# The gate of the embedding as seven products of blocks, with the statistics of the first norm on ScalarE

## The chip, the cores and the metric

The kernel runs on one core of one Trainium2 chip. The metric is the device time of one execution in microseconds; the time of a kernel is the median of its runs. A core has a matrix engine (TensorE, PE in the profile; PEld is its loading of stationary operands), VectorE (DVE), ScalarE (ACT), GpSimd (POOL), and a queue of its own on SyncE (SP). Each engine works through its instructions in the order in which they stand; they wait for each other by semaphores. Transfers run on 16 DMA engines; they are issued here from SP (loads of weights) and POOL (sums of weights in DRAM, small tables, constants).

## The reference

One layer of a decoder on 512 tokens of width 1024, all in float32:

```python
def reference(x, p, w_in, ..., w_up, w_down, w_ple_gate, w_ple, ln2_g, ln2_b, rel_bias):
        m = mixer(x, ...)                                     # three attention branches, gated, projected
        x = layer_norm(DEEPNORM_ALPHA * x + m, ln1_g, ln1_b)  # the first norm
        hid = jax.nn.relu(x @ w_up)                           # 1024 to 4096
        c = jnp.square(hid) @ w_down
        ple = jax.nn.sigmoid(x @ w_ple_gate) * (p @ w_ple)    # the gate of the embedding
        x = layer_norm(DEEPNORM_ALPHA * x + c + ple, ln2_g, ln2_b)
```

The change is about `x @ w_ple_gate` (512 x 1024 times 1024 x 1024) and about the mean and variance of the first norm.

## The kernel before, in words

Every float32 product is made of three matmuls on rounded parts: an operand is split into a high part (a cast on ACT) and a low part (the difference, on DVE), and high x high, high x low and low x high are added up in PSUM. Weights come from DRAM in tiles of 128 x 1024 (512 KB): SP loads a raw tile into a ring of 7 (`fill`, line 179), ACT casts it (`split_next`, line 207), DVE subtracts (line 209) into a ring of 7 high and 7 low tiles. A tile is freed after its last matmul, and `pump` then issues the next splits.

The work is a list of items, written out by hand: each has its weight tiles, a function that issues matmuls into a PSUM bank, and an eviction that is issued with the next item. Between items a function `step` gives each open generator one turn: the attention heads first, later what is in `pending` (the norms and the forms of x). So the length of an item sets how often such a turn comes. The framework then orders the instructions of each engine; that order is fixed when the program is built.

The order of the items is: projections of x, the attention heads beside them, branch projections with their gates, the product of the embedding (`ple_items`), the output projection (`wout_items`, 651 to 697 us), the gate of the embedding (`pleg_items`, 697 to 742 us), and the MLP (`mlp_items`).

The output projection has eight items of 24 matmuls: two halves of the columns, and in each the four token tiles of 128 tokens. The eviction of an item adds the residual (DVE, line 497). After the second half of a token tile its first norm is put into `pending` (`ln1_gen`): statistics by BN_STATS and BN_AGGR on DVE (lines 437, 439), epsilon (441), the power -1/2 on POOL (442), then two passes over each half on DVE (444: subtract the mean and scale by the gain; 446: scale by the power and add the bias). At its next turn it issues eight transposes on TensorE (line 518); ACT evicts them as plain copies (`raws`, line 525) and as the high part of x transposed (line 526), and DVE makes the low part (line 527).

The second norm at the end of the kernel has another form, `layer_norm_act`: the eviction sums as it writes (`accum_out`, line 907), DVE makes the negative mean (454), ACT squares with the mean as its bias and sums (456), DVE scales and adds epsilon (458, 459), POOL takes the power (460), DVE makes the passes (462, 466).

The gate has eight items as well, two column halves by four token tiles, each of 8 x 3 = 24 matmuls of 128 x 128 by 512 columns (lines 564 to 566), with a sigmoid on ACT (570) and a product and a sum on DVE (571, 573). Token tile t is first needed by item t.

The up projection is made of seven products of blocks (of two by two blocks of x and of the weights) instead of eight. It needs sums of blocks of x, made by `x_forms` on DVE and split (lines 664 to 672, 654, 655), and sums of blocks of the weights, `usum`, which transfers in DRAM make beforehand (`sum_steps`, lines 621 and 623, eight steps for each group, issued from POOL). These are spread over the items: from item 24 on one or two an item, each tied to a weight split on DVE four splits back; after the output projection has begun, one every third item. POOL also issues, near 100 to 122 us, the small transfers of the bias tables (`tables`, lines 1011, 1020), which DVE reads later (`turned`, line 1030).

Of the kernel before, what the change touches and what calls it, by code (L numbers as in the profile page):

```python
# [56 lines left out]
def trunk(tc, a, out):  # L57
    nc = tc.nc
    es = ExitStack()
    with es:  # L60
# [99 lines left out]
        def chunk(src, w):  # L160
            return chunk_of(load(src, w))
# [256 lines left out]

        x1 = {}
        x1T = {}  # L420
# [12 lines left out]

        def layer_norm(ts, g, b, fin):
            s6 = one.tile([P, 2, 6], F32, name=nm("bn6"), tag="bn6", bufs=3)
            for h in range(2):
                nc.vector.bn_stats(s6[:, h, :], ts[h])
            mv = small("mv", 2)
            nc.vector.bn_aggr(mv, s6)
            r = small("lr", 1)  # L440
            nc.vector.tensor_scalar(r, mv[:, 1:2], EPS, None, op0=OP.add)
            nc.gpsimd.tensor_tensor(r, r, mhalf, OP.pow)
            for h in range(2):
                nc.vector.scalar_tensor_tensor(ts[h], ts[h], mv[:, 0:1], lnc[g][h], op0=OP.subtract, op1=OP.mult)
            for h in range(2):
                nc.vector.scalar_tensor_tensor(ts[h], ts[h], r, lnc[b][h], op0=OP.mult, op1=OP.add)
                fin(h, ts[h])
# [33 lines left out]
        def wout_items():  # L481
            for half in range(2):
                cs = [chunk(a["wo"][half, c].rearrange("p k n -> p (k n)"), 1024) for c in range(4)]
                for tt in range(4):
# [10 lines left out]
                    def ev(ps, tt=tt, half=half):  # L495
                        y = xn.pop((tt, half))
                        nc.vector.scalar_tensor_tensor(y, y, ALPHA, ps, op0=OP.mult, op1=OP.add)
                        x1[tt, half] = y
                        if half:
                            pending.append(ln1_gen(tt))  # L500
                    item(cs if tt == 3 else [], mm, ev, need=cs)

        def ln1_gen(tt):
            def fin(h, t):
                pass
            layer_norm([x1[tt, 0], x1[tt, 1]], "ln1_g", "ln1_b", fin)
            yield
            q = slice(tt * P, tt * P + P)
            if not x1T:
# [4 lines left out]
                x1T["b"], x1Tl["b"] = bh, bl  # L514
            for h in range(2):
# [4 lines left out]
                t3 = tp.rearrange("p (k t) -> p k t", k=4)  # L520
                for kp in range(2):
# [4 lines left out]
                nc.scalar.copy(o, t3)  # L526
                nc.vector.tensor_sub(x1Tl["b"][:, 4 * h:4 * h + 4, q], t3, o.bitcast(F32))
# [27 lines left out]
        def pleg_items():  # L555
            for half in range(2):
                cs = [chunk(a["wg"][half, c].rearrange("p k n -> p (k n)"), 1024) for c in range(4)]
                for tt in range(4):
                    def mm(ps, tt=tt, cs=cs):
                        for k in range(8):  # L560
                            c = cs[k // 2]
                            s = slice((k % 2) * 512, (k % 2) * 512 + 512)
                            q = slice(tt * P, tt * P + P)
                            nc.tensor.matmul(ps, x1T[k][:, q], c["h"][:, s], start=k == 0, stop=False)
                            nc.tensor.matmul(ps, x1T[k][:, q], c["l"][:, s], start=False, stop=False)  # L565
                            nc.tensor.matmul(ps, x1Tl[k][:, q], c["h"][:, s], start=False, stop=k == 7)  # L566

                    def ev(ps, tt=tt, half=half):
                        g = slot("sg2")
                        nc.scalar.activation(g, ps, AF.Sigmoid)  # L570
                        nc.vector.tensor_mul(g, g, ple.pop((tt, half)))
                        t = x1[tt, half]
                        nc.vector.scalar_tensor_tensor(t, t, ALPHA, g, op0=OP.mult, op1=OP.add)
                        acc[tt, half] = t
                    item(cs if tt == 3 else [], mm, ev, need=cs)
# [14 lines left out]
        ND = 8  # L590
# [1026 lines left out]
```

## Time and profile before

| what | us |
| --- | --- |
| median of three runs (1072.64 to 1073.74) | 1073.5 |
| the profiled execution | 1072.9 |
| its span, first to last instruction | 1071.2 |
| TensorE busy in it | 1060.4 |
| VectorE busy | 705.6 |
| ScalarE busy | 517.5 |
| GpSimd busy | 113.4 |

The profile tells for each engine when an instruction ran, on which line of the kernel it was issued, how long the engine stood idle before it and what ended that wait. A row of the time line has the start, the time from the first to the last of its instructions, the engine, the line, the operation, output and input, the count, and in brackets the idle time and what ended it. Matmuls overlap: a duration is a latency, and the distance between starts is what a matmul costs. Busy time of an engine is an average over stages with different limits.

### The profile page before, as it was taken

How to read it: one execution, taken by the hardware profiler on the slowest of the kernel's cores; microseconds unless marked ns; L12 is line 12 of the kernel's file. 1: busy time of each engine (PE TensorE's matmuls, PEld its weight loads, DVE VectorE, ACT ScalarE, POOL GpSimd, SP SyncE). 2: the span in 40 equal slices, each digit the busy share in tenths (PEclk: the TensorE clock that was granted, in tenths of full speed). 3: DMA queues.
4: the chain of work that ended last, by engine and by line, in shares of the span. 5: the costliest groups of instructions: out<-in, count | busy, mean ns of one | idle time of the engine just before them, and what ended most of it. 6: DMA issues, size and time to landing. Idle time of an engine off the chain costs nothing.

```text
span 1071.2 us, 14785 instructions
## 1 busy us (share of the span) xinstructions
PE 1060.4 (99%) x5562; PEld 910.4 (85%) x5562; DVE 705.6 (66%) x1262; ACT 517.5 (48%) x890; POOL 113.4 (11%) x175
## 2 busy tenths in 40 slices
PE   9999999999999999999999999999999999999996
PEld 6888788999888888888888888888999989989885
DVE  7888667547253757655444453895677877877965
ACT  7665545425232545554333331444765565665741
POOL 0000201011111002122120020110001010000000
PEclk9999999999999999999999999999999999999999
DMA  8332316183767419477897254245889788857502
GB/s 318 126 118 90 117 42 236 50 226 100 222 230 190 164 38 259 156 207 187 270 244 232 99 180 175 99 146 156 284 262 255 254 238 272 237 185 242 190 13 79
DMA packets 56199, 192.43 MB, mean 180 GB/s; under 512 B 7000, under 2 KB 7912, under 8 KB 56128
## 3 DMA queue, kind: packets, MB, share of 16 engines
q1 hardware_dynamic: 35904, 120.51, 32.4%
q0 software_dynamic: 19648, 70.06, 25.4%
q8 instruction: 43, 0.70, 0.3%
q10 hardware_dynamic: 576, 0.92, 0.2%
q14 instruction: 28, 0.23, 0.1%
HBM read 189.34 MB, written 65.04 MB: 237 GB/s over the span
## 4 chain that ended last, share of the span: by engine, by line
PE 96%; DVE 2%; ACT 0%; DMA 0%; issue 0%; SPq 0%; DVEq 0%
PE mm L88 16%; PE mm L89 16%; PE mm L90 16%; PE at L795 4%; PE at L796 4%; PE at L797 4%; PE mm L319 3%; PE mm L321 3%; PE mm L320 3%; PE at L90 1%; PE at L88 1%; PE at L89 1%; PE mm L566 1%; PE mm L493 1%; PE mm L491 1%; PE mm L565 1%
## 5 line engine op out<-in xcount | busy, mean ns | idle before, releaser
L207 ACT CAST wh<-raw 128x1024 fp32r<-128x1024 f32 (+1 forms) x225 | 232.2, 1034 | 310.1 <-PE mm L89 238.8
L209 DVE TENSOR_TENSOR wl<-raw,wh 128x1024 fp32r<-128x1024 f32 (+1 forms) x225 | 269.7, 1203 | 118.9 <-ACT wh L207 114.9
L88 PE MATMUL mm<-xhT,wh 128*128 128x512 f32 x496 | 196.4, 396 | 0.0
L89 PE MATMUL mm<-xlT,wh 128*128 128x512 f32 x496 | 194.0, 391 | 0.0
L90 PE MATMUL mm<-xhT,wl 128*128 128x512 f32 x496 | 194.0, 391 | 0.0
L90 PEld LDWEIGHTS mm<-xhT,wl 128*128 128x128 f32 x496 | 93.2, 188 | 19.6
L88 PEld LDWEIGHTS mm<-xhT,wh 128*128 128x128 f32 x496 | 93.3, 188 | 18.5 <-issue 0.2
L89 PEld LDWEIGHTS mm<-xlT,wh 128*128 128x128 f32 x496 | 93.2, 188 | 18.1 <-issue 0.2
L88 PE MATMUL mm<-x1hT,wh 128*128 128x256 f32 x256 | 73.8, 288 | 0.0
L795 PE MATMUL at<-wh,hh 128*128 128x512 f32 x188 | 73.7, 392 | 0.0
L796 PE MATMUL at<-wl,hh 128*128 128x512 f32 x188 | 73.7, 392 | 0.0
L797 PE MATMUL at<-wh,hl 128*128 128x512 f32 x188 | 73.1, 389 | 0.0
L89 PE MATMUL mm<-x1lT,wh 128*128 128x256 f32 x256 | 72.3, 283 | 0.0
L90 PE MATMUL mm<-x1hT,wl 128*128 128x256 f32 x256 | 71.8, 283 | 0.0
L319 PE MATMUL mm<-wh,xhT 128*128 128x512 f32 x160 | 64.6, 404 | 0.0
L321 PE MATMUL mm<-wh,xlT 128*128 128x512 f32 x160 | 63.1, 395 | 0.0
L320 PE MATMUL mm<-wl,xhT 128*128 128x512 f32 x160 | 62.9, 393 | 0.0
L88 PEld LDWEIGHTS mm<-x1hT,wh 128*128 128x128 f32 x256 | 48.8, 191 | 4.7 <-ACT up L729 2.9
L89 PEld LDWEIGHTS mm<-x1lT,wh 128*128 128x128 f32 x256 | 48.9, 191 | 1.5
L90 PEld LDWEIGHTS mm<-x1hT,wl 128*128 128x128 f32 x256 | 48.6, 191 | 0.0
L621 POOL DMA_DIRECT2D usum<-in_wu_dram x32 | 30.5, 962 | 157.5 <-DVE wl L209 152.7
L797 PEld LDWEIGHTS at<-wh,hl 128*128 128x128 f32 x188 | 35.3, 188 | 7.7
(372 smaller groups left out, 2170.1 us busy)
## 6 DMA issues: line engine op xcount, KB each, us to landing
raw<-in_wt_dram SPq DMA_DIRECT2D x62, 512.0 KB, 4.5
usum<-in_wu_dram POOLq DMA_DIRECT2D x48, 512.0 KB, 8.3
dsum<-in_wd_dram POOLq DMA_DIRECT2D x42, 512.0 KB, 8.5
raw<-usum SPq DMA_DIRECT2D x32, 512.0 KB, 4.7
raw<-dsum SPq DMA_DIRECT2D x28, 512.0 KB, 4.4
raw<-in_wd_dram SPq DMA_DIRECT2D x25, 512.0 KB, 4.6
raw<-in_wu_dram SPq DMA_DIRECT2D x24, 512.0 KB, 5.7
raw<-in_wv_dram SPq DMA_DIRECT2D x20, 512.0 KB, 4.6
```

The lines of the kernel that those rows point to most:

```text
L88: nc.tensor.matmul(ps, wh, xh, start=start, stop=False, skip_group_check=True)
L89: nc.tensor.matmul(ps, wh, xl, start=False, stop=False, skip_group_check=True)
L90: nc.tensor.matmul(ps, wl, xh, start=False, stop=stop, skip_group_check=True)
L207: i = nc.scalar.copy(h, raw)
L209: i = nc.vector.tensor_sub(lo, raw, h.bitcast(F32))
L319: nc.tensor.matmul(ps, x1, c["h"][:, s], start=k == 0, stop=False)
L320: nc.tensor.matmul(ps, x1, c["l"][:, s], start=False, stop=False)
L321: nc.tensor.matmul(ps, x2, c["h"][:, s], start=False, stop=k == 7)
L621: i = nc.gpsimd.dma_start(o, i, accum_op=OP.add, max_dma_last_dim=4096)
L795: nc.tensor.matmul(ps, h[:, q], c["h"][:, s], start=go, stop=False, skip_group_check=True)
L796: nc.tensor.matmul(ps, h[:, q], c["l"][:, s], start=False, stop=False, skip_group_check=True)
L797: nc.tensor.matmul(ps, lo[:, q], c["h"][:, s], start=False, stop=end, skip_group_check=True)
```

## The change

The gate becomes seven products like the up projection's, on the same sums of x. Its weights are laid out in blocks (`wg`), and two groups of sums (`gsum`) join the sums made in DRAM: eight steps each, 16 in all, before those of the up projection. The products run in the order 1, 2, 3, 7, 6, 4, 5; each has two row tiles of 12 matmuls of 512 columns, an item each, and two weight tiles. Products that share a partial sum go on in the same bank; before that ACT copies what the bank holds, and DVE adds the copies up, ahead of the sigmoid and the two DVE operations, which stay as they were. The first norm takes the form of the second (`layer_norm_act`), so BN_STATS and BN_AGGR go. The high and low parts of one quarter of x (first half of the width, last two token tiles) are no longer made and overwritten later: `x_forms` writes the wanted difference there at its end, where `last_form` did it in the up projection. The sums in DRAM start at item 16, with one or two steps an item.

```diff
-        def layer_norm(ts, g, b, fin):
-            s6 = one.tile([P, 2, 6], F32, name=nm("bn6"), tag="bn6", bufs=3)
-            for h in range(2):
-                nc.vector.bn_stats(s6[:, h, :], ts[h])
...
                     def ev(ps, tt=tt, half=half):
                         y = xn.pop((tt, half))
-                        nc.vector.scalar_tensor_tensor(y, y, ALPHA, ps, op0=OP.mult, op1=OP.add)
+                        if not half:
+                            x1sum[tt] = small("lsm", 2)
+                        nc.vector.scalar_tensor_tensor(y, y, ALPHA, ps, op0=OP.mult, op1=OP.add,
+                                                       accum_out=x1sum[tt][:, half:half + 1])
...
-            layer_norm([x1[tt, 0], x1[tt, 1]], "ln1_g", "ln1_b", fin)
+            layer_norm_act([x1[tt, 0], x1[tt, 1]], x1sum[tt], "ln1_g", "ln1_b", fin)()
             yield
...
+                for p, ks, c in ((1, 0, HB), (2, 4, HB), (3, 4, HC), (5, 0, HC)):
+                    forms[p] = [(x1T[k][:, c], x1Tl[k][:, c]) for k in range(ks, ks + 4)]
...
+                plain_too = tt < 2 or h
...
-                nc.scalar.copy(o, t3)
-                nc.vector.tensor_sub(x1Tl["b"][:, 4 * h:4 * h + 4, q], t3, o.bitcast(F32))
+                if plain_too:
+                    nc.scalar.copy(o, t3)
+                    nc.vector.tensor_sub(x1Tl["b"][:, 4 * h:4 * h + 4, q], t3, o.bitcast(F32))
...
         def pleg_items():
...
+            def gate(r, to, g, sign):
+                tt, half = r + 2 * to[1], to[0]
+                nc.scalar.activation(g, g, AF.Sigmoid, scale=sign)
+                nc.vector.tensor_mul(g, g, ple.pop((tt, half)))
+                t = x1[tt, half]
+                nc.vector.scalar_tensor_tensor(t, t, ALPHA, g, op0=OP.mult, op1=OP.add)
+                acc[tt, half] = t
+
+            def operand(p, kp):
+                blk = {1: 0, 2: 1, 4: 3}.get(p)
+                src = a["wg"][kp, blk] if blk is not None else None
+                return chunk(gsum[kp][{5: 0, 6: 1, 7: 2, 3: 3}[p]] if src is None else
+                             src.rearrange("p k n -> p (k n)"), 1024)
+
+            cs = {}
+            for p in (1, 2, 3, 7, 6, 4, 5):
+                name = {1: "x", 6: "x", 5: "x", 7: "y", 4: "y", 2: "z", 3: "w"}[p]
+                for r in range(2):
+                    if not r:
+                        cs[p] = [operand(p, kp) for kp in range(2)]
...
+                    def mm(ps, p=p, r=r):
+                        q = slice(r * P, r * P + P)
+                        for k in range(4):
+                            c = cs[p][k // 2]
+                            n = slice(k % 2 * 512, k % 2 * 512 + 512)
+                            h, lo = forms[p][k]
+                            go, end = k == 0 and p in (1, 2, 3, 7), k == 3 and p in (2, 3, 4, 5)
+                            nc.tensor.matmul(ps, h[:, q], c["h"][:, n], start=go, stop=False, skip_group_check=True)
+                            nc.tensor.matmul(ps, h[:, q], c["l"][:, n], start=False, stop=False, skip_group_check=True)
+                            nc.tensor.matmul(ps, lo[:, q], c["h"][:, n], start=False, stop=end, skip_group_check=True)
+
+                    def ev(ps, p=p, r=r):
+                        if p in (2, 3, 7, 6):
+                            s[p, r] = slot("sg2")
+                            nc.scalar.copy(s[p, r], ps)
+                        if p == 2:
+                            nc.vector.tensor_add(s[2, r], s[2, r], b["x", r])
+                            gate(r, (0, 0), s[2, r], 1.0)
+                        elif p == 4:
+                            nc.vector.tensor_add(s[6, r], s[6, r], ps)
+                            gate(r, (1, 0), s[6, r], -1.0)
+                        elif p == 5:
+                            nc.vector.tensor_add(s[7, r], s[7, r], ps)
+                            gate(r, (1, 1), s[7, r], -1.0)
+                            nc.vector.tensor_add(s[3, r], s[3, r], ps)
+                            gate(r, (0, 1), s[3, r], 1.0)
+                    item(cs[p] if r else [], mm, ev, need=cs[p], bank=bank)
...
+        gsum = [[dram.tile([P, 1024], F32, name=f"gsum{m}_{i}") for i in range(4)] for m in range(2)]
...
-            todo = deque()
+            todo = deque(up_steps(gsum[m], a["wg"][m]) for m in range(2))
             for m in range(ND):
-                todo.append(up_steps(m))
+                todo.append(up_steps(usum[m], a["wu"][m]))
...
-        def last_form():
             for kp in range(2):
-                r = raws[0, 0, kp].rearrange("p (k t) -> p k t", k=2)
+                r = r11[kp].rearrange("p (k t) -> p k t", k=2)
                 h, lo = [x["b"][:, 2 * kp:2 * kp + 2, HC] for x in (x1T, x1Tl)]
                 nc.scalar.copy(h, r)
                 nc.vector.tensor_sub(lo, r, h.bitcast(F32))
...
-            for _ in range((1 + (n % 4 == 0)) if 24 <= n < wout_at - 14 else (n % 3 == 0) if n > wout_at + 4 else 0):
+            for _ in range((1 + (n % 3 == 0)) if 16 <= n < wout_at - 14 else (n % 3 == 0) if n > wout_at + 4 else 0):
                 next(sum_steps_, None)
...
-        "wg": token_major(w_ple_gate[0]),
+        "wg": c(w_ple_gate[0].reshape(2, 2, 2, 128, 2, 512).transpose(1, 4, 0, 3, 2, 5).reshape(2, 4, 128, 2, 512)),
```

More of the change, by code (lines that the diff above doesn't have):

```diff
@@ L555, in pleg_items @@
         def pleg_items():
[L556 to L575, printed above, removed]
@@ L594, in sum_steps, with up_steps @@
         def sum_steps():
-            def up_steps(m):
-                w = [a["wu"][m, i].rearrange("p k n -> p (k n)") for i in range(4)]
-                a1, a2, a3, a4 = usum[m]
+            def up_steps(sums, w):
+                w = [w[i].rearrange("p k n -> p (k n)") for i in range(4)]
+                a1, a2, a3, a4 = sums
                 yield a1, w[2], False
```

32 lines of the change are left out of this document (12 added, 20 removed).

## The prediction

> **What bounds the kernel now.** I read the page first (busy shares and the chain that ended last), then the busy times of two stages, then TensorE's, VectorE's and ScalarE's instructions in order of time around the first norm.
>
> ```profile
> span 1071.2 us, 14785 instructions
> PE 1060.4 (99%) x5562; PEld 910.4 (85%) x5562; DVE 705.6 (66%) x1262; ACT 517.5 (48%) x890; POOL 113.4 (11%) x175
> PE 96%; DVE 2%; ACT 0%; DMA 0%; issue 0%; SPq 0%; DVEq 0%
> ```
>
> ```profile
> 651.20:697.30 46.10, 46.10 (x216) 38.40 (x215) 28.83 (x44) 13.25 (x21) 3.50 (x4) 1.00 0.26 93
> 697.30:742.05 44.75, 44.75 (x204) 36.88 (x202) 34.90 (x51) 20.02 (x35) 3.77 (x5) 1.00 0.38 131
> ```
>
> TensorE is busy 99% of the span and makes 96% of the chain that ended last. The two stage rows (columns: length, then busy time of PE, PEld, DVE, ACT, POOL, granted clock, DMA) are the output projection (651 to 697) and the gate (697 to 742): no idle TensorE in either. So a matmul less is time won one to one, and a TensorE wait is time lost one to one. The question is only which of the two the change makes more of.
>
> ```profile
> 691.00 0.48 PE L491 MATMUL mm<-wh,mh 128*128 128x512 f32 x1
> 696.31 0.40 PE L493 MATMUL mm<-wh,ml 128*128 128x512 f32 x1
> 696.54 1.04 PE L518 MATMUL at<-ident,xn 128*128 128x128 f32 x8
> 697.34 0.47 PE L564 MATMUL mm<-wh,x1hT 128*128 128x512 f32 x1
> 705.17 0.39 PE L565 MATMUL mm<-wl,x1hT 128*128 128x512 f32 x1
> 705.51 0.63 PE L518 MATMUL at<-ident,xn 128*128 128x128 f32 x4
> 706.57 0.48 PE L564 MATMUL mm<-wh,x1hT 128*128 128x512 f32 x1
> ```
>
> An item of 24 matmuls runs from 691.00 to 696.54, so a 512-column matmul takes 5.54 / 24 = 0.23 us (0.227 between starts; the 0.39 shown is its latency), and eight transposes take 697.34 - 696.54 = 0.80. The last row tile's transposes (token tile 3) come at 705.51, where TensorE waits about 0.1 for them.
>
> **The gain.** The gate goes from 8 items of 24 matmuls (192) to 7 products of two row tiles of 12 (168), of the same shape: 24 x 0.227 = 5.4 us less TensorE work.
>
> **What the change adds beside TensorE.**
>
> ```profile
> L207 ACT CAST wh<-raw 128x1024 fp32r<-128x1024 f32 (+1 forms) x225 | 232.2, 1034 | 310.1 <-PE mm L89 238.8
> L209 DVE TENSOR_TENSOR wl<-raw,wh 128x1024 fp32r<-128x1024 f32 (+1 forms) x225 | 269.7, 1203 | 118.9 <-ACT wh L207 114.9
> L571 DVE TENSOR_TENSOR sg<-sg,ple 128x512 f32<-128x512 f32 x8 | 5.5, 690 | 9.7 <-ACT sg L570 9.7
> L437 DVE BATCH_NORM_STATS2 bn<-xn 128x6 f32<-128x512 f32 x5 | 3.5, 690 | 0.1
> usum<-in_wu_dram POOLq DMA_DIRECT2D x48, 512.0 KB, 8.3
> ```
>
> Weight tiles of the gate go from 8 to 14: six more casts (6 x 1.03 = 6.2 us ACT), six more splits (6 x 1.2 = 7.2 DVE) and six more loads on SP's queue, each behind a buffer that a split seven places earlier sets free, so issued well ahead of use. Eight additions of partial sums cost 8 x 0.69 = 5.5 on DVE, and eight copies out of PSUM some 8 x 0.65 = 5.2 on ACT (the 0.65 of a cast of that size, row 692.38 below); eight BN_STATS (5.5) leave DVE. A product that goes on in a bank waits for the copy of what the bank held; between the two stand the 12 matmuls of the other row tile, 2.7 us, as cover for 0.65 of copy. Were ACT behind by more than 2 us there, each such wait would show one to one. DVE was busy 34.9 of the gate's 44.75 us, and ACT 20.0, so neither becomes the bound by its total; their cost is in the order of the queues, below. Sixteen more DRAM sums pass POOL's queue, from item 16 on instead of 24, some of them ahead of the bias tables' small transfers. That I cost at nothing:
>
> ```profile
> 118.72 3.14 POOL L1020 DMA_DIRECT2D sh<-rv  x4
> L1030 DVE COPY shf<-sh x8: 418/420/498, 161.9 to 334.2; 128x512 f32<-128x512 f32 x8
> ```
>
> The tables are issued by 118.72 + 3.14 = 121.9 and first read at 161.9. Four sums of 8.3 us ahead of them, one after the other, would be 33 us of those 40. The cover is 7 us at that pessimistic count; if it were gone, DVE would stand at the copy and TensorE after it. The gate's own sums are finished long before 697, and the up projection's last sums stand at least 26 weight splits ahead of their use in the built order, where it was 17. Bounds of these transfers: 0 to 3 us.
>
> **The loss: the first norm's chain gets longer, and its transposes are wanted sooner.** Both parts come from the change. The only undisturbed case of the new norm (sum by accumulation, squares on ACT) is the second norm at the end of the kernel; VectorE, ScalarE, POOL, VectorE:
>
> ```profile
> 1046.02 0.69 DVE L907 SCALAR_TENSOR_TENSOR xn<-xn,mm 128x512 f32<-128x512 f32 x1 [0.61 <-PE mm L899]
> 1046.75 0.21 DVE L454 TENSOR_SCALAR lnm<-lsm 128x1 f32<-128x1 f32 x1
> 1047.00 0.72 ACT L456 ACTIVATE junk<-xn,lnm 128x512 f32<-128x512 f32 x1 [5.69 <-DVE lnm L454]
> 1047.85 0.73 ACT L456 ACTIVATE junk<-xn,lnm 128x512 f32<-128x512 f32 x1
> 1048.70 0.21 DVE L458 TENSOR_SCALAR lr<-lsq 128x1 f32<-128x1 f32 x1
> 1049.49 0.15 DVE L459 TENSOR_SCALAR lr<-lr 128x1 f32<-128x1 f32 x1
> 1049.71 0.55 POOL L460 TENSOR_TENSOR lr<-lr,mhalf 128x1 f32<-128x1 f32 x1 [6.36 <-DVE lr L459]
> 1050.29 1.41 DVE L466 SCALAR_TENSOR_TENSOR xn<-xn,lr,ln_b 128x512 f32<-128x512 f32 x2 [0.66 <-POOL lr L460]
> ```
>
> From the eviction to the first half being written: 1050.29 + 0.75 - 1046.02 = 5.0 us. The old norm, undisturbed (token tile 0):
>
> ```profile
> 678.60 0.69 DVE L497 SCALAR_TENSOR_TENSOR xn<-xn,mm 128x512 f32<-128x512 f32 x1 [2.71 <-PE mm L493]
> 681.69 1.41 DVE L446 SCALAR_TENSOR_TENSOR xn<-xn,lr,ln_b 128x512 f32<-128x512 f32 x2
> 684.04 0.69 DVE L497 SCALAR_TENSOR_TENSOR xn<-xn,mm 128x512 f32<-128x512 f32 x1 [0.34 <-PE mm L493]
> 690.41 0.69 DVE L497 SCALAR_TENSOR_TENSOR xn<-xn,mm 128x512 f32<-128x512 f32 x1 [0.76 <-PE mm L493]
> 698.79 2.35 DVE L209 TENSOR_TENSOR wl<-raw,wh 128x1024 fp32r<-128x1024 f32 x2
> 701.07 1.28 DVE L527 TENSOR_TENSOR x1lT<-at,x1hT 128x512 fp32r<-128x512 f32 x2
> 690.84 0.65 ACT L525 COPY x1r<-at 128x256 f32<-128x256 f32 x2 [4.18 <-PE at L518]
> 692.38 0.65 ACT L526 CAST x1hT<-at 128x512 fp32r<-128x512 f32 x1
> ```
>
> 681.69 + 0.75 - 678.60 = 3.8 us. The new one is 1.2 longer, and it goes through ScalarE twice, whose queue holds other work. The walk by token tile, on the clock of the profile before, in the built order of the changed program:
>
> Tile 0: evicted at 678.60, ready at 683.6 and, its second half, 684.3; wanted at 683.85. About 0.2 us of waiting.
> Tile 1: evicted at 684.4. Its squares stand on ACT behind the six transpose evictions of tile 0, which end about 686.6 (690.84 to 693.0 is 2.2 us in the rows for tile 1), 1.5 us later than they could start: ready near 690.7 where the slot is 690.3. With the second half 0.6 us.
> Tile 2: evicted at 691.2. Squares behind tile 1's evictions (to 693.4), a cast of 1.0 between the two squares, and on DVE one split (1.14 between starts) ahead of the scale and one more after it: 693.4 + 0.85 + 1.0 gives a split at 695.3 to 696.4; 0.8 for the scale, 1.1 for the other split and 0.75 for the last pass put the first half at 699.3. TensorE ended the projection at 697.3 (696.54 plus the waits so far). 2.0, and 0.3 between the halves: 2.3 us.
> Tile 3: evicted at 699.8, as soon as DVE is through with tile 2. Then two splits (2.3) and a subtraction (0.6) stand on DVE ahead of the mean: 703.4. From there the rows above: squares 1.8 with their start, 0.8 and 0.8 to the last pass (707.0), 0.75 more: 707.8. Its transposes stood 35 matmuls into the gate; since norm steps are emitted once an item and an item is now half as long, they stand behind 12. TensorE leaves tile 2's at 699.3 + 0.3 + 0.8 = 700.4 and gets there at 700.4 + 12 x 0.227 and 0.1 for the change from transposes to matmuls, 703.2. It waits 4.6, and 0.3 for the second half: 4.9 us.
>
> Nothing passes an instruction that waits on TensorE's queue, so product 1's second row tile, and all after it, stand behind these transposes. Later there is no new wait: the second half of product 1 and products 2 and 3 (5 x 12 x 0.227 = 13.6 us) lie between tile 3's transposes and product 7, which needs the sums of x: four subtractions and two splits (6 x 0.69 = 4.1 us of DVE), among other work.
>
> Sum of the waits: 0.2 + 0.6 + 2.3 + 4.9 = 8.0; less the 5.4 of matmuls and the 0.2 that TensorE lost at tile 3 before (705.17 to 706.57 is 1.40, of which two matmuls and eight transposes fill 1.25): **+2.4 us**. Ends for the unknown parts: POOL's power took 0.55 with DVE waiting and 1.0 in the old norm, where DVE worked beside it:
>
> ```profile
> 680.54 1.00 POOL L442 TENSOR_TENSOR lr<-lr,mhalf 128x1 f32<-128x1 f32 x1 [8.29 <-DVE lr L441]
> ```
>
> In tiles 0, 1 and 3 DVE now waits for it, as in the tail, so I take 0.55; with 1.0 everywhere three chains grow by 0.45, +3.6 in all. At the other end, if no split stood in a chain, tile 2 would cost nothing and tile 3, ready 5.0 after an eviction at 697.4, about 2: -3 us. The order of the queues is fixed in the program, so I stay at the walk. The profiled run took 1072.9 for its span of 1071.2; the median shown is 1073.5, 0.6 above, and the forecast goes on the median: 1075.9.
>
> **Rivals.**
> 1. The TensorE clock falls in the long wait. Rows by stretch at the end, after the last matmul:
>
> ```profile
> 1062.17 0.28 PE L899 MATMUL at<-wh,hl 128*128 128x256 f32 x1
> 1066.00:1067.00 1.00, 0.00 (x0) 0.00 (x0) 0.81 (x3) 0.00 (x0) 0.00 (x0) 1.00 0.11 43
> 1067.00:1068.00 1.00, 0.00 (x0) 0.00 (x0) 0.00 (x0) 0.00 (x0) 0.00 (x0) 0.82 1.01 356
> 1.26 4.02 PE L965 MATMUL at<-zero 128*128 128x512 bf16 x9 [1.26 <-DVE zero L962]
> ```
>
> The grant fell at about 1067.6, 5.2 us after TensorE went quiet at 1062.45; a wait of 4.6 falls short of that one case, but not by much. The price: the first nine matmuls took 4.02 us, 0.45 each against 0.23 later, so a slow stretch of such a length costs about 2.0 us, an estimate: 1077.9. I give it less than an even chance, for the 4.6 against 5.2. [...]
> 2. Faster: the chains do not collide. If the splits of tiles 2 and 3 end early, for instance because their order on DVE costs less than the walk has it, the wait at tile 3 falls to about 2 and the time to 1073.5 - 3 = 1070.5. It decides once the waits are below 5.4 + 0.2 = 5.6 us together. Against it: the old kernel's rows show the same two splits and subtractions taking 698.79 to 702.3 in front of tile 3's norm.
> 3. The two cancel: waits of 3.5 to 7.7 us by another split of the walk, and the time within 0.2% of before (about 2.1 us, what a measurement of this kernel can tell from none).
> 4. The sums at items 16 to 24 delay the tables or the first weights: +1 to +3 on top, 1077 to 1079.
>
> **Chances.** The walk holds 0.62 (its own range 1075.0 to 1077.2; three tenths of it lie under the bound of 0.2%, 1075.65), rival 1 0.18, rival 2 0.08, rival 3 0.07, rival 4 0.05. Slower: 0.43 of the walk, 0.18 and 0.05, together 0.66; same: 0.19 of the walk and 0.07, 0.26; faster 0.08. The range 1073.0 to 1079.0 leaves out rival 2 and the far end of rival 1.
>
> **What would show it.** Right: in the profile after, transposes of the first norm with TensorE idle before them, about 2 us after the projection and 4 to 5 us one product into the gate, both ended by the last pass of the norm on DVE; 24 fewer 512-column matmuls; no other idle TensorE. Wrong: the waits under 5 us together, a granted clock below 1.00 near 708, or new idle time near 160 where the tables are read.

## The result, and the profile after

The changed kernel takes 1076.4 us (median of 7 runs, 1074.9 to 1077.2) against 1073.2 for the kernel before on the same chip (7 runs, 1072.5 to 1073.7): a ratio of 1.0029, 95% interval 1.0017 to 1.0040, so 3.2 us slower. The profiled execution took 1076.1, its span is 1074.2.

The page of the changed kernel, with its span, busy times and the engines' shares of the chain that ended last:

```profile
span 1074.2 us, 14824 instructions
PE 1058.4 (99%) x5538; PEld 907.7 (84%) x5538; DVE 711.6 (66%) x1278; ACT 533.4 (50%) x918; POOL 123.1 (11%) x191
PE 94%; DVE 3%; issue 1%; ACT 1%; DMA 0%; POOL 0%; SPq 0%; DVEq 0%; POOLq 0%
```

There are 24 matmuls fewer, but PE's busy time falls by 2.0 us only, and the span grows by 3.0. The same two stages as in the prediction, output projection and gate (length, busy time of PE, PEld, DVE, ACT, POOL, granted clock, DMA share, GB/s):

```profile
651.62:697.77 46.15, 45.91 (x209) 37.33 (x207) 23.85 (x45) 16.60 (x32) 2.58 (x4) 1.00 0.26 82
697.77:746.38 48.61, 43.62 (x186) 35.72 (x185) 41.93 (x58) 31.04 (x51) 6.16 (x8) 0.93 0.76 220
```

Before, TensorE was never idle here and the clock was 1.00. Now the gate has 48.61 - 43.62 = 5.0 us of idle TensorE, and a mean clock of 0.93: two losses, not one. (The granted clock is a share of TensorE's full speed; at 0.50, called the half clock below, a matmul takes about twice as long: 0.43 us against 0.227 below.) TensorE's instructions in order of time show where:

```profile
697.54 0.39 PE L483 MATMUL mm<-wh,ml 128*128 128x512 f32 x1
700.09 1.38 PE L513 MATMUL at<-ident,xn 128*128 128x128 f32 x8 [2.17 <-DVE xn L456]
...
701.94 0.63 PE L593 MATMUL at<-wh,x1lT 128*128 128x512 f32 x1
...
704.92 0.42 PE L591 MATMUL at<-wh,x1hT 128*128 128x512 f32 x1
...
705.42 0.40 PE L593 MATMUL at<-wh,x1lT 128*128 128x512 f32 x1
708.55 1.94 PE L513 MATMUL at<-ident,xn 128*128 128x128 f32 x8 [2.73 <-DVE xn L456]
710.14 0.78 PE L591 MATMUL at<-wh,x1hT 128*128 128x512 f32 x1
...
711.91 0.40 PE L592 MATMUL at<-wl,x1hT 128*128 128x512 f32 x1
...
746.38 0.28 PE L88 MATMUL mm<-x1hT,wh 128*128 128x256 f32 x1
```

L513 are the transposes of the first norm: tile 2 at 700.09, behind the projection, and tile 3 at 708.55, behind the 12 matmuls of product 1's first row tile. Both wait for the norm's last pass on VectorE (L456). From 701.94 to 704.92 seven matmuls start 0.43 us apart instead of 0.227. The same time in windows that lie between the changes of the granted clock:

```profile
698.20:701.50 3.30, 1.31 (x9) 1.10 (x10) 2.84 (x6) 1.57 (x3) 1.05 (x1) 1.00 0.97 247
701.60:704.90 3.30, 3.30 (x9) 2.55 (x8) 2.70 (x4) 1.61 (x4) 0.84 (x1) 0.50 0.99 286
705.00:708.30 3.30, 0.82 (x4) 0.33 (x2) 2.34 (x5) 0.97 (x4) 0.56 (x1) 1.00 0.94 212
708.50:711.70 3.20, 3.15 (x12) 2.89 (x13) 2.19 (x4) 1.82 (x6) 0.00 (x0) 0.50 0.54 165
711.90:715.00 3.10, 3.10 (x15) 2.57 (x14) 3.10 (x6) 2.81 (x4) 0.00 (x0) 1.00 0.00 0
```

Full, half, full, half, full: a window with TensorE mostly idle (busy for 1.31 and for 0.82 of 3.30 us) is each time followed by one at 0.50. Why tile 3 is late is in VectorE's order:

```profile
700.62 0.68 DVE L489 SCALAR_TENSOR_TENSOR xn<-xn,mm 128x512 f32<-128x512 f32 x1
701.22 2.36 DVE L209 TENSOR_TENSOR wl<-raw,wh 128x1024 fp32r<-128x1024 f32 x2
703.50 0.68 DVE L525 TENSOR_TENSOR x1lT<-at,x1hT 128x512 fp32r<-128x512 f32 x1
704.10 0.20 DVE L444 TENSOR_SCALAR lnm<-lsm 128x1 f32<-128x1 f32 x1
705.18 0.75 DVE L452 SCALAR_TENSOR_TENSOR xn<-xn,lnm,ln_g 128x512 f32<-128x512 f32 x1 [0.89 <-ACT junk L446]
...
707.65 1.42 DVE L456 SCALAR_TENSOR_TENSOR xn<-xn,lr,ln_b 128x512 f32<-128x512 f32 x2 [0.68 <-POOL lr L450]
```

Eviction (700.62), two weight splits and a subtraction, and only at 704.10 the mean; the last pass starts at 707.65, where the prediction's walk has 707.0; 0.4 of the difference is that this profile's output projection starts later than before's.

One length serves for all comparisons below: from the first matmul of the output projection to the first of the up projection, here called the stage. Before it is 742.05 - 651.20 = 90.85 us, after 746.38 - 651.62 = 94.76, so +3.91. That is more than the 3.2 by which the time grew; the rest is in the experiments' last part.

### The profile page after: what moved, and what is told of

It reads as the page before. It is cut to its first block, busy times and chain, and to the rows that moved or that the text cites. A ratio compares the mean times of both kernels' runs of the same rounds, so it can differ in the third digit from the quotient of the medians.

```text
span 1074.2 us, 14824 instructions
## 1 busy us (share of the span) xinstructions
PE 1058.4 (99%) x5538; PEld 907.7 (84%) x5538; DVE 711.6 (66%) x1278; ACT 533.4 (50%) x918; POOL 123.1 (11%) x191
## 4 chain that ended last, share of the span: by engine, by line
PE 94%; DVE 3%; issue 1%; ACT 1%; DMA 0%; POOL 0%; SPq 0%; DVEq 0%; POOLq 0%
PE mm L88 16%; PE mm L89 16%; PE mm L90 16%; PE at L820 4%; PE at L821 4%; PE at L822 4%; PE mm L319 3%; PE mm L321 3%; PE mm L320 3%; PE at L90 1%; PE at L89 1%; PE at L88 1%; PE at L591 1%; PE at L593 1%; PE at L592 1%
## 5 line engine op out<-in xcount | busy, mean ns | idle before, releaser
L207 ACT CAST wh<-raw 128x1024 fp32r<-128x1024 f32 (+1 forms) x231 | 238.4, 1034 | 310.4 <-PE mm L89 236.9
L209 DVE TENSOR_TENSOR wl<-raw,wh 128x1024 fp32r<-128x1024 f32 (+1 forms) x231 | 277.1, 1204 | 118.7 <-ACT wh L207 114.6
L657 POOL DMA_DIRECT2D usum<-in_wu_dram x32 | 28.1, 881 | 192.6 <-DVE wl L209 177.9
```

The source lines that it names most:

```text
L207: i = nc.scalar.copy(h, raw)
L209: i = nc.vector.tensor_sub(lo, raw, h.bitcast(F32))
L657: i = nc.gpsimd.dma_start(o, i, accum_op=OP.add, max_dma_last_dim=4096)
```

## The experiments

Theory A is the prediction's: 24 matmuls less, against waits that the longer norm and the earlier transposes make together, and, as the profile after adds, a half clock behind the waits. The rivals: the norm alone makes the loss (B), the gate's extra work makes it (C), the new gate gives less than 5.4 us (D), the DRAM sums cost something (the prediction's rival 4), or VectorE's queue isn't what holds tile 3. The table has the profiled stage and the median of 5 to 11 runs with the kernel before beside them (1073.1 to 1073.2 each time).

| kernel | stage, us | against before | time, us | ratio to before (95%) |
|---|---|---|---|---|
| before | 90.85 | | 1073.2 | |
| changed | 94.76 | +3.91 | 1076.4 | 1.0029 (1.0017 to 1.0040) |
| new gate, old norm | 92.19 | +1.34 | 1073.2 | 1.0002 (0.9993 to 1.0012) |
| old gate, new norm | 92.58 | +1.73 | 1074.9 | 1.0016 (1.0007 to 1.0025) |
| changed, waits filled | 93.45 | +2.60 | 1074.7 | 1.0015 (1.0007 to 1.0024) |
| changed, tile 3 one item later | 94.18 | +3.33 | 1075.4 | 1.0017 (1.0008 to 1.0025) |
| changed, one split moved | 94.22 | +3.37 | 1075.7 | 1.0023 (1.0014 to 1.0032) |
| old norm, wait filled | 90.23 | -0.62 | 1071.4 | 0.9985 (0.9977 to 0.9994) |
| old norm, one item later | 87.83 | -3.02 | 1069.3 | 0.9968 (0.9955 to 0.9980) |
| the same, wait filled | 87.82 | -3.03 | 1069.6 | 0.9966 (0.9953 to 0.9978) |
| old norm, three items later | | | 1074.4 | 1.0007 (0.9998 to 1.0016) |
| before, early and added sums | 90.83 | -0.02 | 1072.4 | 0.9994 (0.9984 to 1.0003) |
| before, early sums | 90.83 | -0.02 | 1073.6 | 1.0001 (0.9992 to 1.0010) |

### One half of the change alone

The new gate with the old norm, against the changed kernel:

```
+        def layer_norm(ts, g, b, fin):
...
-                        nc.vector.scalar_tensor_tensor(y, y, ALPHA, ps, op0=OP.mult, op1=OP.add,
-                                                       accum_out=x1sum[tt][:, half:half + 1])
+                        nc.vector.scalar_tensor_tensor(y, y, ALPHA, ps, op0=OP.mult, op1=OP.add)
...
-            layer_norm_act([x1[tt, 0], x1[tt, 1]], x1sum[tt], "ln1_g", "ln1_b", fin)()
+            layer_norm([x1[tt, 0], x1[tt, 1]], "ln1_g", "ln1_b", fin)
```

> The changed kernel with the statistics of the first norm back on VectorE; gate and sums of x stay in the new order. Theory A (gain of 24 matmuls, less the waits for the norm's transposes, which the longer chain and the earlier demand make together): the old chain took 3.8 us from a tile's eviction to its scaled half against 5.0, so TensorE keeps up at tiles 0 to 2, and only tile 3, still wanted 12 matmuls into the gate, makes it wait, about 5 us, because two splits and a subtraction of the up projection stand on VectorE ahead of its norm. -5.4 + 5.3 - 0.2 = -0.3; if the wait halves the TensorE clock as at 708 in the changed kernel, +1.3 more: 1073 to 1074.5. Rival B (the norm on ScalarE makes the whole loss): no wait beyond 1 us is left and the gain shows: about 1068. Rival C (the gate's own extra work makes it: sums earlier, more splits): the time stays at the changed kernel's, 1076.4.

Measured: 1073.2, no difference from before. TensorE's transposes of tile 3 in this kernel, and the busy times and the clock around them:

```profile
704.88 1.94 PE L525 MATMUL at<-ident,xn 128*128 128x128 f32 x8 [4.57 <-DVE xn L451]
```

```profile
699.30:702.60 3.30, 1.02 (x5) 0.51 (x3) 3.23 (x6) 0.05 (x1) 0.81 (x1) 1.00 1.00 238
702.80:706.00 3.20, 1.12 (x6) 1.15 (x7) 2.60 (x4) 0.00 (x0) 0.99 (x1) 0.50 1.05 315
706.10:709.40 3.30, 3.30 (x11) 2.72 (x10) 2.99 (x5) 2.72 (x7) 0.00 (x0) 0.50 0.89 262
```

One wait only, of 4.57 us (700.31 to 704.88), and the clock at half for two stretches, from 702.66, inside the wait, to 709.48. Without the new norm too, the wait and the clock eat more than the gain: the stage is 1.34 longer than before. That the time is the same has to do with a shorter end of the program, the experiments' last part.

The `layer_norm` put in is the one of the kernel before. The other half: the new statistics in the kernel before.

```
-                        nc.vector.scalar_tensor_tensor(y, y, ALPHA, ps, op0=OP.mult, op1=OP.add)
+                        if not half:
+                            x1sum[tt] = small("lsm", 2)
+                        nc.vector.scalar_tensor_tensor(y, y, ALPHA, ps, op0=OP.mult, op1=OP.add,
+                                                       accum_out=x1sum[tt][:, half:half + 1])
...
-            layer_norm([x1[tt, 0], x1[tt, 1]], "ln1_g", "ln1_b", fin)
+            layer_norm_act([x1[tt, 0], x1[tt, 1]], x1sum[tt], "ln1_g", "ln1_b", fin)()
```

> The kernel before with only the new statistics of the first norm. Theory A: each chain is 1.2 us longer, but tile 3 is wanted 35 matmuls into the gate instead of 12, 5 us later; waits of a few tenths at each of the four tiles, some 1.5 us in all, against 0.2 before: 1074 to 1075. Rival B (the norm makes the whole loss of the changed kernel, 3.2 + 5.4 = 8.6 us): about 1082. Rival C: 1073.2, as before.

Measured: 1074.9, +1.73 in the stage. The windows of this kernel around the end of the projection show idle TensorE of 0.37 and 0.38 us, in waits of a few tenths, at full clock:

```profile
690.00:700.00 10.00, 9.63 (x46) 7.29 (x45) 8.45 (x15) 7.36 (x14) 2.65 (x4) 1.00 0.23 79
700.00:715.00 15.00, 14.62 (x71) 11.90 (x72) 13.11 (x23) 6.87 (x18) 0.93 (x1) 1.00 0.46 158
```

B falls: the norm alone costs 1.7 us, not 8.6. C falls as the whole cause: without the new norm the time is 1073.2, where C has 1076.4. The new norm costs 3.91 - 1.34 = 2.6 us in the new gate and 1.7 in the old one, so part of the loss belongs to neither half alone.

### What the clock costs

The changed kernel, with matmuls that nothing reads in the two waits, written to the bank that the transposes fill next:

```
             for h in range(2):
                 tp = at_bank()
+                for _ in range({2: 8, 3: 18}.get(tt, 0) if not h else 0):
+                    nc.tensor.matmul(tp, x1T[0][:, 0:P], busy["c"]["h"][:, 0:512], start=True, stop=True,
+                                     skip_group_check=True)
```

> The changed kernel with 26 added matmuls of 128x512 that nothing reads: 8 (1.8 us) ahead of the transposes of tile 2 and 18 (4.1 us) ahead of those of tile 3, in the time that TensorE waits for the norm, into the bank that the transposes write next. They leave the waits' ends where they are and keep TensorE working in them. If the half clock after the waits (701.6 to 705.0 and 708.4 to 711.8 in the changed kernel) has a price of its own, the clock stays at 1.00 there and the time falls by about 1.3 us, to 1075.1; the first slow stretch only shortens the second wait and costs nothing. If the clock costs nothing, 1076.4 or, where the added matmuls overrun the wait, up to 1 us more.

TensorE in this kernel (L514 are the added matmuls, L517 the transposes), then the window behind tile 3's transposes:

```profile
699.62 1.38 PE L517 MATMUL at<-ident,xn 128*128 128x128 f32 x8 [0.35 <-DVE xn L457]
...
703.59 4.24 PE L514 MATMUL at<-wh,x1hT 128*128 128x512 f32 x18
707.99 1.38 PE L517 MATMUL at<-ident,xn 128*128 128x128 f32 x8 [0.16 <-DVE xn L457]
```

```profile
708.00:711.30 3.30, 3.20 (x18) 2.62 (x19) 2.81 (x5) 2.54 (x7) 0.00 (x0) 1.00 0.61 185
```

Tile 3's transposes start 707.99 - 651.14 = 56.85 us after the projection's first matmul, 56.93 in the changed kernel: the waits end where they did. The clock stays at 1.00, the transposes take 1.38 instead of 1.94, and the stage is 94.76 - 93.45 = 1.31 us shorter, with 26 matmuls more. That is the price of the half clock in the changed kernel. Only its second stretch is paid for: the first slowed matmuls that had to wait for tile 3 anyway, which is why the profile names 2.73 us of idle there where the walk had 4.6. With the clock out of the way the stage is +2.60, and the prediction's sum was +2.4.

The same in the new gate with the old norm, for tile 3 only:

```
+                for _ in range({3: 18}.get(tt, 0) if not h else 0):
+                    nc.tensor.matmul(tp, x1T[0][:, 0:P], busy["c"]["h"][:, 0:512], start=True, stop=True,
...
```

> The new gate with the old norm, and 18 added matmuls of 128x512 (4.1 us) that nothing reads in the wait of 4.6 us for tile 3. The wait's end stays; the clock stays at 1.00, so that the transposes take 1.0 instead of 1.9 and the first eight matmuls behind them 0.23 instead of 0.43 each: 0.9 + 8 x 0.2 = 2.5 us at most, 1070.7 to 1071.5. If the clock has no price: 1073.2.

Measured: 1071.4, the stage 92.19 - 90.23 = 1.96 us shorter. More work lay in the half clock there: from 704.88, where tile 3's transposes start, to 709.48 it is 4.60 us, against 708.55 to 711.80, 3.25 us, in the changed kernel.

### The place of tile 3's transposes

One line moves them by whole items; first in the changed kernel:

```
             yield
+            for _ in range(1 if tt == 3 else 0):
+                yield
             q = slice(tt * P, tt * P + P)
```

> The changed kernel with the transposes of token tile 3 one item (one row tile, 12 matmuls, 2.7 us) later. Theory A: the wait for tile 3 falls by what TensorE now does first, from some 4.9 us at full clock to about 2.4 with the wait for tile 2 left at 2.3: 2.7 us less, and no second slow stretch behind it (1.3 us): 1072.5 to 1074. A theory that puts the loss on the norm's work on ScalarE and VectorE and not on the place of the transposes expects 1076.4 still.

Measured: 1075.4, 0.58 us less in the stage where 2.7 and more was expected. A miss. VectorE's instructions in order of time, in this kernel, and TensorE's transposes of tile 3 show why:

```profile
707.47 0.14 DVE L449 TENSOR_SCALAR lr<-lr 128x1 f32<-128x1 f32 x1
708.98 1.23 DVE L209 TENSOR_TENSOR wl<-raw,wh 128x1024 fp32r<-128x1024 f32 x1 [1.36 <-ACT wh L207]
710.12 1.41 DVE L456 SCALAR_TENSOR_TENSOR xn<-xn,lr,ln_b 128x512 f32<-128x512 f32 x2
711.01 1.29 PE L515 MATMUL at<-ident,xn 128*128 128x128 f32 x8 [1.80 <-DVE xn L456]
```

A weight split (708.98) now stands between the step ahead of the power (707.47) and the last pass, and itself waits for a cast. The norm became ready 1.8 us later, so TensorE waited 1.80 at tile 3 after all, and in this execution the clock fell after each of the two waits (0.50 from 702 to 705 and from 713 to 715). It took 1076.1, the longest of the eleven; the four shortest (1073.0 to 1074.2) had a granted clock of 0.996 or 0.997, the other seven 0.995. So the stage in the table is this kernel at its worst, and the median falls by 1.0.

The same edit with the old norm, in the kernel with the new gate:

```
             layer_norm([x1[tt, 0], x1[tt, 1]], "ln1_g", "ln1_b", fin)
             yield
+            for _ in range(1 if tt == 3 else 0):
+                yield
```

> The new gate with the old norm on VectorE and the transposes of token tile 3 one item (12 matmuls, 2.7 us) later. Theory A: the wait of 4.6 us for tile 3 that the new gate with the old norm showed (700.3 to 704.9) is filled by those 12 matmuls down to about 2.0: 1073.2 - 2.7 = 1070.5, and up to 2.2 us less where the shorter wait no longer halves the clock (half from 702.7 to 709.5 in that kernel); 1068.5 to 1070.5, faster than both kernels. Rival D (the new gate gives less than 24 x 0.227 = 5.4 us of TensorE, the wait being a symptom): no better than 1072.5.

Tile 3's transposes here:

```profile
704.91 1.29 PE L527 MATMUL at<-ident,xn 128*128 128x128 f32 x8 [1.85 <-DVE xn L451]
```

Measured: 1069.3, 0.32% faster than before and the fastest kernel of this study. Tile 3 is ready when it was (704.91 against 704.88); TensorE does 12 matmuls first and waits 1.85 instead of 4.57. D falls: it has no better than 1072.5, and the stage is 3.02 shorter with 1.85 us of idle TensorE still in it, together 4.9 of the 5.4. With 9 added matmuls in the rest of the wait (`{3: 9}` in the lines shown above for 18):

> As the kernel with the old norm and tile 3 one item later, with 9 added matmuls of 128x512 (2.0 us) that nothing reads in the wait that is left. If that wait still halves the clock in some executions, this is faster by up to 2 us and its runs lie closer together; if not, the same time within 0.5 us.

Measured: 1069.6, the same within the runs' spread (1068.7 to 1071.8 without them, 1069.1 to 1069.8 with them). In the profiled execution without them the clock stayed at 1.00 from 700 to 713.

Three items later (`range(3 if tt == 3 else 0)`):

> As with the old norm, the transposes of tile 3 three items (36 matmuls, 8.2 us) later, where the kernel before has them by time. No wait for the norm is left. But only 13.6 - 8.2 = 5.4 us of matmuls then lie between them and the first product that needs the sums of x, whose making starts with those transposes: evictions on ScalarE (2.2), a cast (0.6), and on VectorE four subtractions and two splits (4.1). Theory A: the waits move there, some 4 to 6 us, and the gain of 5.4 is gone again: 1073 to 1075. Rival (any place behind the norm's end is as good): 1068 to 1069.

This is further back than the kernel before has them: behind 48 matmuls of the gate, not 35, and 709.02 - 651.87 = 57.15 us into the stage, where before has 705.51 - 651.20 = 54.31. The two longest waits of TensorE in this kernel, in order of time, then the clock around the first of them:

```profile
718.51 0.56 PE L605 MATMUL at<-wh,t3h 128*128 128x512 f32 x1 [2.18 <-ACT t3h L700]
...
727.14 0.39 PE L88 MATMUL mm<-x1hT,wh 128*128 128x256 f32 x1 [1.13 <-ACT wh L207]
```

```profile
715.39:718.80 3.41, 1.23 (x6) 0.72 (x5) 3.41 (x6) 3.10 (x5) 0.65 (x1) 1.00 0.92 267
718.80:722.22 3.42, 3.42 (x9) 2.28 (x9) 3.42 (x6) 0.69 (x2) 0.15 (x1) 0.50 0.93 267
```

Measured: 1074.4. No wait for the norm, but 2.2 us for the operand made from a sum of x (t3h) with a half-clock stretch behind it, then 1.1 for a weight cast on ScalarE, the engine that makes those operands too. (The matmul at 727.14 is one of four of the up projection that run inside the gate here, so the table gives no stage for this kernel.) So the place of tile 3's transposes has a cost on either side, and the gate as changed has it too early: with the old norm one item later is better and three are too many. Two items later was not run.

### VectorE's queue ahead of tile 3

The changed kernel, with no new chunk prepared at the item where tile 3's splits came up:

```
-            pump(freed, {1: 3, 3: 0, 4: 0}.get(n, 1 if n < 10 else 2))
+            pump(freed, {1: 3, 3: 0, 4: 0, wout_at + 16: 0}.get(n, 1 if n < 10 else 2))
```

> The changed kernel with the next weight chunk's preparation asked for one item later, which puts one of the two weight splits ahead of tile 3's mean behind it, into the 0.9 us in which VectorE waits there for the squares on ScalarE. The prediction's step for tile 3 had both splits on the way to its transposes. If that is so, they come 1.0 us earlier (a split takes 1.14 between starts): 1075.4, with 0.3 more or less for where the clock's stretches fall. If VectorE's queue is not what holds tile 3 back: 1076.4.

VectorE around tile 3's mean, and TensorE's transposes of tiles 2 and 3:

```profile
702.85 0.20 DVE L444 TENSOR_SCALAR lnm<-lsm 128x1 f32<-128x1 f32 x1
702.97 1.22 DVE L209 TENSOR_TENSOR wl<-raw,wh 128x1024 fp32r<-128x1024 f32 x1
704.10 0.75 DVE L452 SCALAR_TENSOR_TENSOR xn<-xn,lnm,ln_g 128x512 f32<-128x512 f32 x1
```

```profile
699.65 1.38 PE L513 MATMUL at<-ident,xn 128*128 128x128 f32 x8 [2.15 <-DVE xn L456]
...
707.30 1.29 PE L513 MATMUL at<-ident,xn 128*128 128x128 f32 x8 [3.52 <-DVE xn L456]
```

One split now runs behind the mean. The transposes start 707.30 - 651.21 = 56.09 us into the stage, 0.84 earlier than in the changed kernel; 1.0 was expected. The median falls by 0.7, inside the spread of these runs (1074.2 to 1078.3), so the verdict, that VectorE's queue holds tile 3 back, rests on that row of one profile; the time doesn't contradict it. The wait it names, 3.52, is longer than the changed kernel's 2.73 although it ends earlier: here the clock was full in front of it. Idle time alone would have been misread.

### The DRAM sums, and an end that got shorter

The kernel before with the changed kernel's sums; the 16 added ones nothing reads:

```
+        gsum = [[dram.tile([P, 1024], F32, name=f"gsum{m}_{i}") for i in range(4)] for m in range(2)]
...
-            todo = deque()
+            todo = deque(up_steps(gsum[m], a["wg"][m]) for m in range(2))
...
-            for _ in range((1 + (n % 4 == 0)) if 24 <= n < wout_at - 14 else (n % 3 == 0) if n > wout_at + 4 else 0):
+            for _ in range((1 + (n % 3 == 0)) if 16 <= n < wout_at - 14 else (n % 3 == 0) if n > wout_at + 4 else 0):
```

> The kernel before with the changed kernel's DRAM sums alone: 16 more software DMAs for two blocks of gate weights, and all sums from item 16 at the higher rate. The gate and the norm are those of before, the added sums are read by nobody. Rival 4 (the sums delay the tables or the first weights, and so make part of the loss): 1074 to 1076, with idle TensorE near 160 or in the start-up. Against it: the sums cost nothing, 1073.1. The time from the last pass of the last norm to the end, 1.1 us shorter in every kernel with the new gate than in the two with the old one, is also seen here: 3.3 instead of 4.4 if these DMAs bring it, and then 1072.0.

Measured: 1072.4, the stage unchanged (-0.02). Rival 4 falls; in the changed kernel itself TensorE was busy 210.00 of the 210 us from 120 to 330, where the tables are read. But the end is different. The last pass of the last norm on VectorE, first of the kernel before (span 1071.2), then of the changed kernel (1074.2), then of this one (1070.2):

```profile
1065.27 1.53 DVE L943 SCALAR_TENSOR_TENSOR xn<-xn,lr,ln_b 128x512 f32<-128x512 f32 x3
```

```profile
1069.35 1.53 DVE L968 SCALAR_TENSOR_TENSOR xn<-xn,lr,ln_b 128x512 f32<-128x512 f32 x3
```

```profile
1065.61 1.54 DVE L944 SCALAR_TENSOR_TENSOR xn<-xn,lr,ln_b 128x512 f32<-128x512 f32 x3
```

From its end to the span's end it is 1071.2 - 1066.80 = 4.4 us before, 1074.2 - 1070.88 = 3.3 after, and 1070.2 - 1067.15 = 3.05 here. The old gate with the new norm has 4.4, the new gate with the old norm 3.2. The output's transfers land 2.0 to 2.1 us after their issue in all three, so the difference lies behind them. To tell the added DMAs from the earlier schedule, the last two lines of the edit were also made alone:

> The kernel before with its own DRAM sums from item 16 on at the higher rate, and no added ones. In the kernel with early and added sums the end after the last pass of the last norm was 1.3 us shorter than before (3.05 against 4.4 us) and the time 0.7 lower. If the schedule brings that, 1072.4 and 3.1 us here too; if the 16 added DMAs bring it, 1073.1 and 4.4.

Measured: 1073.6. The span of its profiled execution is 1072.4, the last pass ends at 1068.05, and the end is 4.35. So the shorter end comes with the 16 added software DMAs. Why the end should depend on them was not found.

## Why the prediction came out

The time was put at 1075.9 and measured at 1076.4. The direction, the places of the waits and their sum were right. That the number came so near is partly luck: what happened was the walk together with rival 1, and two terms that the sum left out, the clock (+1.31) and a shorter end (-1.1), nearly cancelled.

- **The gain, 5.4.** Right, as far as the runs show it: 4.9 of it where the waits are short, in the stage with the old norm one item later.
- **Waits of 8.0, less the 0.2 of before.** Right in place and in sum. Tiles 0 to 2: 2.17 us at tile 2 as idle before the first half (2.0 in the walk), tenths at tiles 0 and 1. Tile 3, with both of the causes that the walk named: two splits and a subtraction ahead of its mean (moving one split brought it 0.84 forward), and transposes 12 instead of 35 matmuls into the gate (12 matmuls more, with the old norm, are worth 4.4 us of stage, and 90.23 - 87.82 = 2.4 where the waits are filled and the clock is kept up in both). The net +2.4 was measured as +2.60 where the clock is kept up. As idle time the profile after names less, 2.17 + 2.73 = 4.9 us and some tenths, which by its number alone touches the prediction's sign of being wrong (under 5 us): the half clock filled part of the second wait. The upper end of the walk, three chains longer by 0.45 each, comes to +3.75 by its own terms, not +3.6.
- **The clock, costed at nothing in the sum.** Wrong: this is the term that failed. Rival 1 had the fall of the clock and a price of 2.0 us, but at a chance of 0.18, because the one fall of the clock in the trace of before came 5.2 us after TensorE went quiet, and I took a wait of 4.6 as short of it. Waits of 2.17 and 2.73 us were enough; the price was 1.31 (and 1.96 in the new gate with the old norm). The prediction's own sign of being wrong, a granted clock below 1.00 near 708, is in the windows. The tail's 5.2 was no bound from below: it told when the clock fell, not how little idle time would do. Cut into the stretches of 3.41 us that the last section counts off, that tail is one stretch still busy for 1.64 us, with no fall behind it, and one idle throughout, with the fall at its end:

```profile
1060.81:1064.22 3.41, 1.64 (x14) 1.44 (x12) 3.34 (x10) 0.00 (x0) 0.11 (x1) 1.00 0.41 154
1064.22:1067.63 3.41, 0.00 (x0) 0.00 (x0) 2.59 (x5) 0.00 (x0) 0.88 (x1) 1.00 0.22 80
```

- **Sums at no cost.** Right for the stage (-0.02). Not foreseen was that the added DMAs come with an end 1.1 us shorter. From the first up-projection matmul to the last matmul the changed kernel also takes 1066.25 - 746.38 = 319.87 instead of 1062.17 - 742.05 = 320.12; why is open.
- **VectorE and ScalarE no bound by their totals.** Right: in the gate VectorE was busy 41.9 of 48.6 us, and it was its order that counted.
- **Rivals.** Waits below 5.6 us (rival 2) did not occur, but the condition was right: with the old norm one item later they are, and that kernel is 3.8 us faster than before. Rivals 3 and 4 did not happen.

Summed over the profiled executions: the stage +3.91 (2.60 of waits less matmuls, 1.31 of clock), the later stages -0.25, the end -1.1, and a start that was 0.4 later. That start is not put down to the change: in kernels with the same sums in DRAM the projection's first matmul lies anywhere from 651.14 to 652.26. The four make 3.0, the difference of the spans.

## What to carry to other kernels

A change that takes work off the bounding engine also brings forward everything emitted by item: count anew how much work stands between a late operand's producer and its consumer, on the producer's queue too. Here the new gate was worth 0.3% and became a loss because one tile's transposes came too early and the norm ahead of them got longer; with the shorter norm and the transposes one item later, it is a gain. Where TensorE is the bound, price a wait of a few microseconds at its length, and look in the granted clock for a half-clock stretch behind it: here waits of 2.17 and 2.73 us had one of 3.41 us each, and the price was 1.31 us (1.96 in the new gate with the old norm). Read idle time and granted clock together: here the wait at tile 3 was 2.73 us behind a stretch at 0.50, and 3.52, though it ended 0.84 us earlier, where the clock in front of it was 1.00.

## What the hardware showed that was not expected

The clock's changes in the changed kernel lie at about 701.56, 704.97, 708.39 and 711.80 (worked out from the mean clock of short windows that hold one change each), 3.41 us apart, and in the new gate with the old norm at 702.66 and 709.48, twice that. The next fall in the changed kernel is at its end, at 1070.20 (a mean clock of 0.60 from 1070 to 1071). That is 368.64 us behind the first, or 108 times 3.4133. So within each of these two profiles the changes lie whole multiples of 3.41 us apart, but they don't fall on the same times in both: 702.66 is 1.10 behind 701.56. The stretches below are counted off from a change in steps of 3.4133; where no change is near, their edges are an estimate.

The stretches in front of the two falls in the changed kernel were not idle throughout: TensorE was busy for 1.31 of 3.30 and 0.82 of 3.30 us by the windows above. Waits of nearly the same length went both ways: 1.80 (tile 3 one item later) and 2.17 us (changed) were followed by a half clock, while 1.85 (old norm one item later) and the 2.15 at tile 2 (one split moved) were not. Cut at the stretches, the profiles show a difference. First three stretches of the kernel with one split moved, counted back from its fall at about 708.69; then two of the old norm one item later, counted back 105 stretches from its fall at 1062.22:

```profile
698.45:701.86 3.41, 2.11 (x13) 1.74 (x14) 3.02 (x5) 1.69 (x6) 0.36 (x1) 1.00 0.71 240
701.86:705.27 3.41, 1.92 (x9) 1.25 (x7) 3.17 (x7) 1.98 (x5) 0.85 (x1) 1.00 0.59 178
705.27:708.69 3.42, 1.35 (x10) 1.14 (x11) 2.18 (x5) 0.71 (x3) 0.56 (x1) 1.00 0.88 139
```

```profile
700.41:703.82 3.41, 2.65 (x12) 1.88 (x10) 3.34 (x7) 1.77 (x2) 1.66 (x2) 1.00 0.98 247
703.82:707.24 3.42, 2.29 (x14) 1.90 (x15) 3.42 (x5) 1.97 (x6) 0.05 (x1) 1.00 1.07 291
```

The waits of 2.15 (697.50 to 699.65) and 1.85 us (703.06 to 704.91) lie across an edge, and each side keeps 2.11 us of work or more (695.03 to 698.45, the other side of the first, has 2.46): no fall. The wait of 3.52 (703.78 to 707.30) lies across one too; its first side is busy for 1.92, its second for 1.35, and the fall comes behind the second. In the windows of 3.1 to 3.5 us printed in this document, TensorE was busy for at most 1.35 us in those that a half clock followed, and for 1.64 or more in those at full clock that none followed. The stretch before the second fall of tile 3 one item later (708.81 to 712.22) has about 1.6 us, so no bound can be read off between the two.

Part of that work is transposes: the stretch 698.45 to 701.86 above has matmuls for 1.1 us at most, the rest of its 2.11 is float32 transposes, and the clock stayed at 1.00 behind it, while it fell to 0.50 behind 1.23 us of matmuls without transposes (three items later, above).

The kernels with such waits also spread more from run to run: over 3 us for tile 3 one item later (1073.0 to 1076.1, the shortest at a granted clock of 0.997, the longest at 0.995), and over 0.8 with the waits filled (1074.3 to 1075.2). That this comes from where the stretches lie against the waits is an estimate that no run shows.
